# Hybrid decoder step: key norms of sets 1 to 3 by a block of ones and wide reciprocals instead of token-major sums and transpositions

## The chip, the cores and the metric

One Trainium2 chip, one core. The metric is device time in microseconds (us), the median of a few runs.

Engines are named as in the profile: PE multiplies matrices (PEld is its loading of the stationary operand), DVE is the vector engine, ACT the scalar engine, POOL the general-purpose one, SP issues DMAs. Each works through its own list of instructions in order, so an instruction that waits holds up those behind it.

## What is computed

One layer of a decoder for 2048 new tokens and 32 sample tokens (8 sequences of 4), model width 1024, 16 heads of 64 channels. A convolution branch and an RWKV-7 branch share one normalised input. The change is in the RWKV branch, in the keys, which are scaled to unit length per head and token:

```python
kk = (k_f * k_k).reshape(hs)
kk = kk / jnp.maximum(jnp.sqrt(jnp.sum(kk * kk, axis=-1, keepdims=True)), 1e-12)
k_h = (k_f * (1.0 + (a - 1.0) * k_a)).reshape(hs)
...
def step(S, inp):
    r_t, k_t, v_t, d_t, kk_t, a_t = inp
    sa = jnp.einsum('bhvk,bhk->bhv', S, -kk_t)
    S = (S * d_t[:, :, None, :] + sa[..., None] * (kk_t * a_t)[:, :, None, :]
         + v_t[..., None] * k_t[:, :, None, :])
```

`kk` occurs twice in a step, so the kernel multiplies by one over the sum of squares once, in one of the two places.

## The kernel before

**Tiling.** The tokens are cut into four sets of 512 (`th` = 0 to 3). Set 3 (`LAST`) also carries the 32 sample tokens, so its tiles have 544 columns. Channels lie on the 128 partitions, tokens in the columns. A pair `p` = 0 to 7 is two heads, 128 channels. So there are 32 pairs of set and heads, worked one after the other.

**Main stream.** The projections of a set are blocks of 24 matrix products each (`proj`, lines 266 to 276): every fp32 operand is split into a high and a low part of type fp32r, and high times high, low times high and high times low are summed in a PSUM bank called `ip`. In the trace these are `ip<-XH,whl` and `ip<-XL,whl`, one record each. Other products of fp32 operands show as two records each, but for transpositions, which show as one.

**Sides.** For each pair there are generators that run beside the main stream, a piece at a time: `rwkv_keys` (line 808: decays, norms, scaled keys `BK`, receptances `AR`, bonus `bv`), `rwkv_solve` (inverts the triangles `X` of all eight chunks in a chain of small DVE operations), `rwkv_merge`, `rwkv_load`, then `rwkv_chain` (line 1091: eight chunks in series, each PE `pa`, DVE `us`, PE `pb<-us`, DVE and ACT `SV`, PE `pb<-SV`, DVE `S`) and `rwkv_out`. The keys of pair k run while the chain of pair k-1 does.

**What sets the order.** `drive` (line 351) takes a product of the main stream, and then lets each side emit its next pieces where three things hold: its share of the window given to it is due, its inputs and PSUM banks are ready by a modelled clock (class `Clock`, the cost of an instruction in `Traced.cost`, line 130 on), and, for sides not urgent, the modelled DVE is at most 1.8 us ahead of the modelled PE (`BACKLOG`). A `yield` of a side gives the weight of the piece, what its next piece must wait for, and how many banks it needs. So all five engines' orders are fixed when the program is built, and a new cost in the model or a new `yield` can move every piece behind it.

**The norms before.** The squares `sq` (line 821) are multiplied as the stationary operand, 128 tokens at a time, with a two-column matrix `bone2` (line 826). This gives the sums of the two heads with tokens on partitions: `ss`, 128x8. DVE clips and inverts these few numbers (lines 827, 828). Later ACT spreads them over 64 columns each (line 876), PE transposes the four blocks back to channels on partitions (line 880), and DVE multiplies `ta` by them out of PSUM (line 881). In set 3 the 32 sample tokens go the same way apart (lines 829 to 833 and 882 to 889). The matrix `bones` (128x128, ones in two 64x64 blocks) is already there for the bonus (lines 921, 922).

**Buffers.** `tmp` is a pool of 8 tiles of 128x576, shared by the main stream and the sides (line 403); `pt` has two PSUM banks (line 406), `ip` three.

Of the kernel before, what the change touches and what calls it, by code (L numbers as in the profile page):

```python
# [7 lines left out]
F32 = mybir.dt.float32  # L8
F32R = mybir.dt.float32r
BF16 = mybir.dt.bfloat16  # L10
AF = mybir.ActivationFunctionType
ALU = mybir.AluOpType
# [4 lines left out]
P = 128  # L17
# [5 lines left out]
NT = NCH * C  # L23
# [3 lines left out]
W = {"sq": 1.0, "norm": 1.0, "lora": 2.0, "one": 1.0, "scan": 2.0, "exp": 2.0, "key": 1.0, "bones": 1.5,  # L27
     "sv": 1.5, "bt": 2.0, "score": 4.0, "inv0": 5.0, "inv": 0.45, "inv1": 4.0, "merge": 2.0,
     "gk": 1.3, "us": 1.3, "sa": 1.3, "state": 1.3, "samp": 2.0, "gn": 4.0, "out": 2.0}
# [81 lines left out]
class Traced:  # L111
# [18 lines left out]
    def cost(self, op, out, ins, k):  # L130
        n = out.free_size()
        if self.name == "PE":
            if op == "transpose":
                return 109.0
            lhs, rhs = k["lhsT"], k["rhs"]
            if rhs.dtype == F32R:
                mode, t = (P, P), 8 + 0.45 * n
            else:
                part = [next(x for x in (32, 64, 128) if v <= x) for v in (lhs.ap[0][1], lhs.free_size())]
                mode, t = tuple(part), 2 * max(0.84 * max(lhs.free_size(), n), 26.0) / (1 if part == [P, P] else 1.9)  # L140
            t += 170 * (mode != self.clock.mode)
            self.clock.mode = mode
            return t
        if self.name == "DVE":
            per = {"transpose": 1.6, "tensor_tensor_scan": 2.1}.get(op, 1.05)
            if op == "tensor_reduce":
                n = ins[0].free_size()
            return 150 + per * n
        if self.name == "ACT":
            return 200 + 0.84 * n + 90 * max(0, len(ins) - 1)  # L150
        if k.get("op") == ALU.pow:
            return 1650.0
        return 120 + 2.3 * n if op == "tensor_tensor" else 120 + 1.0 * n
# [26 lines left out]
def hybrid_kernel(tc, x_prompt, x_sample, state_conv, state_shift, state_rwkv, norm_g, w_in, conv_w,  # L180
# [5 lines left out]
    V, A, G, T = (Traced(e, n, clock) for e, n in ((nc.vector, "DVE"), (nc.scalar, "ACT"), (nc.gpsimd, "POOL"), (nc.tensor, "PE")))  # L186
# [7 lines left out]
    NSAMP = NS * SL  # L194
# [7 lines left out]
    TW = NT + 64  # L202
# [165 lines left out]
    TPS = NT // P  # L368
# [34 lines left out]
    tmp = ph1.enter_context(tc.tile_pool(name="tmp", bufs=8))  # L403
    ep = ph1.enter_context(tc.tile_pool(name="ep", bufs=2))
    sm = ph1.enter_context(tc.tile_pool(name="sm", bufs=2))
# [399 lines left out]
    def cview(t):  # L805
        return t[:, 0:NT].rearrange("p (c t) -> p c t", t=C)

    def rwkv_keys(th, p, o):

        lt = cur["lora"]  # L810
# [8 lines left out]

        sq = tmp.tile([P, TW], F32, name="tmp")  # L820
        A.activation(out=sq[:, 0:nt], in_=kT[:, 0:nt], func=AF.Square, scale=vc("kk", p))
        yield W["sq"], [sq[:, 0:nt]], 1 + samp
        pt = new_pt([P, 512], F32, name="pt")
        ss = sm.tile([P, 2 * TPS + 2], F32, name="ss")
        for j in range(TPS):
            T.matmul(pt[:, 2 * j:2 * j + 2], lhsT=sq[:, j * P:(j + 1) * P], rhs=bone2, start=True, stop=True)
        V.tensor_scalar(out=ss[:, 0:2 * TPS], in0=pt[:, 0:2 * TPS], scalar1=1e-24, scalar2=None, op0=ALU.max)
        V.reciprocal(ss[:, 0:2 * TPS], ss[:, 0:2 * TPS])
        if samp:
            pt = new_pt([P, 512], F32, name="pt")  # L830
            T.matmul(pt[0:NSAMP, 0:2], lhsT=sq[:, n:nt], rhs=bone2, start=True, stop=True)
            V.tensor_scalar(out=ss[0:NSAMP, 2 * TPS:], in0=pt[0:NSAMP, 0:2], scalar1=1e-24, scalar2=None, op0=ALU.max)
            V.reciprocal(ss[0:NSAMP, 2 * TPS:], ss[0:NSAMP, 2 * TPS:])
        yield W["norm"], [up], 2


        L = tmp.tile([P, TW], F32, name="tmp")
# [33 lines left out]
        kh = tmp.tile([P, TW], F32, name="tmp")  # L871
        A.activation(out=kh[:, 0:nt], in_=ta[:, 0:nt], func=AF.Identity, scale=kah[:, p:p + 1], bias=kai[:, p:p + 1])
        V.scalar_tensor_tensor(out=ta[:, 0:nt], in0=ta[:, 0:nt], scalar=1.0, in1=Pi[:, 0:nt], op0=ALU.add, op1=ALU.mult)

        sb = tmp.tile([P, TW], F32, name="tmp")
        A.copy(sb[:, 0:NT].rearrange("p (a d) -> p a d", d=64), ss[:, 0:2 * TPS].unsqueeze(2).broadcast_to([P, 2 * TPS, 64]))
        yield W["key"], [sb[:, 0:NT]], 1
        pt = new_pt([P, 512], F32, name="pt")
        for j in range(TPS):
            T.transpose(pt[:, j * P:(j + 1) * P], sb[:, j * P:(j + 1) * P], ident)  # L880
        V.tensor_tensor(out=ta[:, 0:n], in0=pt, in1=ta[:, 0:n], op=ALU.mult)
        if samp:
            sb = tmp.tile([P, TW], F32, name="tmp")
            A.copy(sb[0:NSAMP, 0:P].rearrange("p (a d) -> p a d", d=64),
                   ss[0:NSAMP, 2 * TPS:].unsqueeze(2).broadcast_to([NSAMP, 2, 64]))
            yield 0.0, [sb[0:NSAMP, 0:P]], 1
            pt = new_pt([P, 512], F32, name="pt")
            T.transpose(pt[:, 0:NSAMP], sb[0:NSAMP, 0:P], ident[0:NSAMP, 0:NSAMP])
            V.tensor_tensor(out=ta[:, n:nt], in0=pt[:, 0:NSAMP], in1=ta[:, n:nt], op=ALU.mult)
        yield W["key"]  # L890
        V.tensor_tensor(out=kh[:, 0:nt], in0=kh[:, 0:nt], in1=kT[:, 0:nt], op=ALU.mult)
        yield W["key"]
# [730 lines left out]
```

## Time and profile before

| what | value |
|---|---|
| median of 3 runs | 3192.13 us (3189.84 to 3195.04) |
| the profiled execution | 3193.32 us |
| its span, first to last instruction | 3191.6 us |
| mean granted PE clock | 0.992 |
| records on PE, DVE, ACT | 21530, 5704, 2571 |

The page's second part shows the span in 40 slices; a digit is the busy share in tenths:

```profile
PE   7999999999999999999999999999999999999998
PEld 6777777887777778877777789989889889778896
DVE  5687777776666666666666676766677664443332
ACT  5454445444333434434443334344444432211201
POOL 2011111111000001100101010000000000000000
```

Set 0 ends in the ninth slice, set 3 begins near the 24th, and from the 34th on the output products run without the sides. PE shows a 9 nearly everywhere, the others never do. In a row of the timeline stand the start, the duration, the engine, the operation, and output and inputs by name; an idle time in front of it and who ended it follow in brackets. Matrix products overlap at their ends, so what one costs is read from the distance between starts.

### The profile page before, as it was taken

Reading aid. Unit: us, or ns where it says so; the run is one execution under the profiler, and the core shown is the slowest. Engines: PE = TensorE matmul, PEld = TensorE weight load, DVE = VectorE, ACT = ScalarE, POOL = GpSimd, SP = SyncE. Lnnn points to the kernel's source line nnn. Section 1 sums busy time; section 2 is a strip of 40 time slices with the busy share of each in tenths; the row PEclk is TensorE's granted clock in tenths of the full one; section 3 lists DMA queues with packets and bytes.
Section 4 is the critical chain, followed back from the end, with each engine's and each line's share of the span. In section 5 each row is a group of like instructions: output and inputs, shape, how many; then the busy total and the mean of one; then the engine's idle time right before and its main releaser. Section 6 shows DMA issues by size and latency. Waiting matters only on the chain.

```text
span 3191.6 us, 55625 instructions
## 1 busy us (share of the span) xinstructions
PE 3092.0 (97%) x21530; PEld 2596.5 (81%) x21530; DVE 1992.5 (62%) x5704; ACT 1241.9 (39%) x2571; POOL 309.6 (10%) x517
## 2 busy tenths in 40 slices
PE   7999999999999999999999999999999999999998
PEld 6777777887777778877777789989889889778896
DVE  5687777776666666666666676766677664443332
ACT  5454445444333434434443334344444432211201
POOL 2011111111000001100101010000000000000000
PEclk9999999999999999999999999999999999999999
DMA  8786666644444444444444444434443469988863
GB/s 267 258 267 220 213 212 220 207 173 148 146 162 160 155 159 159 169 157 153 159 153 158 159 147 142 138 127 139 144 143 135 138 223 318 363 337 304 316 241 120
DMA packets 241504, 615.09 MB, mean 193 GB/s; under 512 B 33931, under 2 KB 143620, under 8 KB 187479
## 3 DMA queue, kind: packets, MB, share of 16 engines
q1 hardware_dynamic: 241094, 611.00, 55.8%
q8 instruction: 170, 2.79, 0.4%
q14 instruction: 96, 0.78, 0.1%
q0 software_dynamic: 144, 0.52, 0.0%
HBM read 452.10 MB, written 159.36 MB: 192 GB/s over the span
## 4 chain that ended last, share of the span: by engine, by line
PE 69%; DVE 18%; ACT 5%; issue 5%; DMA 3%; POOL 1%; SPq 0%; ACTq 0%; DVEq 0%; POOLq 0%
PE ip L121 49%; PE pt L121 10%; PE po L121 6%; PE pb L121 3%; DVE X L121 2%; DVE tmp L121 2%; DVE tt L121 2%; ACT tmp L121 2%; DVE Mi L121 2%; DVE whl L121 1%; DVE us L121 1%; PE pa L121 1%; DVE S L121 1%; DMA wraw<-in_w_in_dram 1%; ACT Xbd L121 1%
## 5 line engine op out<-in xcount | busy, mean ns | idle before, releaser
L121 PE MATMUL ip<-XH,whl 128*128 128x512 f32 (+3 forms) x7776 | 2105.1, 351 | 6.6 <-DVE gt L121 3.9
L121 PEld LDWEIGHTS ip<-XH,whl 128*128 128x128 f32 x7776 | 1342.0, 190 | 178.3 <-issue 27.5
L121 PE MATMUL ip<-XL,whl 128*128 128x512 f32 (+3 forms) x3888 | 1364.0, 351 | 2.7 <-POOL XL L121 2.6
L121 PEld LDWEIGHTS ip<-XL,whl 128*128 128x128 f32 x3888 | 738.5, 190 | 79.0 <-issue 7.0
L121 DVE TENSOR_TENSOR X<-X,tt 128x60 f32<-128x60 f32 (+24 forms) x992 | 211.7, 213 | 27.5
L121 DVE TENSOR_TENSOR tt<-Mi,X 128x60 f32<-128x60 f32 (+24 forms) x992 | 209.9, 212 | 27.4
L121 DVE SCALAR_TENSOR_TENSOR S<-pb,pe,sp 64x64 f32<-64x64 f32 x512 | 143.8, 281 | 106.6 <-PE pb L121 100.5
L121 ACT ACTIVATE sp<-S,pe 128x128 f32<-128x128 f32 x256 | 99.5, 400 | 244.7 <-DVE S L121 241.2
L121 ACT ACTIVATE tmp<-ip,vec 128x512 f32<-128x512 f32 (+2 forms) x174 | 103.2, 593 | 231.6 <-PE ip L121 230.2
L121 ACT COPY SV<-pb 64x64 f32<-64x64 f32 x256 | 53.3, 208 | 329.2 <-DVE SV L121 325.5
L121 DVE TENSOR_TENSOR whl<-wraw,whl 128x1024 fp32r<-128x1024 f32 x105 | 134.2, 1279 | 58.0 <-ACT whl L121 57.7
L121 PE MATMUL po<-whl,MH 128*128 128x512 f32 x544 | 170.4, 394 | 0.0
L121 DVE TENSOR_TENSOR us<-pa,P 64x64 f32<-64x64 f32 x512 | 110.2, 215 | 45.2 <-PE pa L121 33.7
L121 PEld LDWEIGHTS pb<-us,Xbd 128*128 128x128 f32 x512 | 85.9, 189 | 56.9 <-PE ip L121 21.5
L121 PE MATMUL ip<-RH,whl 128*128 128x512 f32 (+2 forms) x512 | 128.4, 341 | 1.7 <-DMA whl<-w_or 1.6
L121 PEld LDWEIGHTS pb<-SV,BKt 128*128 128x128 f32 x512 | 85.1, 189 | 54.6 <-ACT SV L121 45.9
L121 ACT CAST whl<-wraw 128x1024 fp32r<-128x1024 f32 x105 | 109.5, 1044 | 50.5 <-DMA wraw<-in_w_out_r_dram 14.8
L121 PE MATMUL pb<-SV,BKt 128*128 128x128 f32 x512 | 107.3, 291 | 17.4 <-ACT SV L121 17.3
L121 DVE TENSOR_TENSOR GM<-pt,mask_p 128x512 f32<-128x512 f32 x128 | 82.4, 685 | 64.4 <-PE pt L121 64.4
L121 PEld LDWEIGHTS po<-whl,MH 128*128 128x128 f32 x544 | 102.2, 188 | 24.0 <-DVE whl L121 0.3
L121 PE MATMUL pb<-us,Xbd 128*128 128x64 f32 x512 | 90.1, 258 | 23.7 <-DVE us L121 23.1
L121 ACT COPY Xbd<-Xo 32x256 f32<-32x256 f32 x128 | 88.1, 688 | 64.0 <-DVE Xo L121 61.9
(494 smaller groups left out, 3838.6 us busy)
## 6 DMA issues: line engine op xcount, KB each, us to landing
wraw<-in_w_in_dram SPq DMA_DIRECT2D x81, 512.0 KB
whl<-w_k SPq DMA_DIRECT2D x24, 1024.0 KB
whl<-w_r SPq DMA_DIRECT2D x24, 1024.0 KB
whl<-w_v SPq DMA_DIRECT2D x24, 1024.0 KB
whl<-w_z SPq DMA_DIRECT2D x24, 1024.0 KB
whl<-w_xin SPq DMA_DIRECT2D x24, 1024.0 KB
whl<-w_cg SPq DMA_DIRECT2D x24, 1024.0 KB
whl<-w_zc SPq DMA_DIRECT2D x24, 1024.0 KB
```

What stands on the lines that cost most here:

```text
L121: r = f(*a, **k)
```

## The change

In set 0 the norms stay as they were (`norms_narrow`). From set 1 on (`norms_wide`) the squares are split into an fp32r high part `sh` and a low part `sl`, both are multiplied with `bones`, which gives each channel the sum of its own head's squares, ACT copies the result to SBUF (`ri`), and DVE inverts all 128x512 (544 in set 3) numbers, in pieces of 128 columns. The final multiplication then reads SBUF. The 32 sample tokens need no path of their own. The model of the clock gets a price for the reciprocal.

```diff
+            if op == "reciprocal":
+                per = 6.0
             return 150 + per * n
...
+    def ones_product(pt, h, l, c0, c1, out):
+
+        T.matmul(pt[:, 0:c1 - c0], lhsT=bones, rhs=h[:, c0:c1], start=True, stop=False)
+        T.matmul(pt[:, 0:c1 - c0], lhsT=bones, rhs=l[:, c0:c1], start=False, stop=True)
+        A.copy(out[:, c0:c1], pt[:, 0:c1 - c0])
+
+    def norms_wide(sq, sg, nt, o):
+
+        sh = tmp.tile([P, TW], F32R, name="tmp")
+        A.copy(sh[:, 0:nt], sq[:, 0:nt])
+        yield W["sq"], [sh[:, 0:nt]]
+        sl = tmp.tile([P, TW], F32R, name="tmp")
+        V.scalar_tensor_tensor(out=sl[:, 0:nt], in0=sq[:, 0:nt], scalar=1e-36, in1=sh[:, 0:nt].bitcast(F32),
+                               op0=ALU.max, op1=ALU.subtract)
+        yield W["sq"], [sl[:, 0:nt]], len(sg)
+        ri = tmp.tile([P, TW], F32, name="tmp")
+        for (c0, c1) in sg:
+            ones_product(new_pt([P, 512], F32, name="pt"), sh, sl, c0, c1, ri)
+        yield W["norm"], [ri[:, 0:nt]]
+        for c0 in range(0, nt, P):
+            c1 = min(nt, c0 + P)
+            V.reciprocal(ri[:, c0:c1], ri[:, c0:c1])
+            yield W["norm"] / 2
+        o["ri"] = ri
...
-        yield W["sq"], [sq[:, 0:nt]], 1 + samp
-        pt = new_pt([P, 512], F32, name="pt")
-        ss = sm.tile([P, 2 * TPS + 2], F32, name="ss")
-        for j in range(TPS):
-            T.matmul(pt[:, 2 * j:2 * j + 2], lhsT=sq[:, j * P:(j + 1) * P], rhs=bone2, start=True, stop=True)
-        V.tensor_scalar(out=ss[:, 0:2 * TPS], in0=pt[:, 0:2 * TPS], scalar1=1e-24, scalar2=None, op0=ALU.max)
-        V.reciprocal(ss[:, 0:2 * TPS], ss[:, 0:2 * TPS])
...
-        yield W["norm"], [up], 2
+        if th:
+            yield from norms_wide(sq, sg, nt, o)
+        else:
+            yield from norms_narrow(sq, o)
+        yield 0.0, [up], 2
...
+        if "ri" in o:
+            yield W["key"]
+            V.scalar_tensor_tensor(out=ta[:, 0:nt], in0=o["ri"][:, 0:nt], scalar=1e24, in1=ta[:, 0:nt], op0=ALU.min, op1=ALU.mult)
+        else:
+
             sb = tmp.tile([P, TW], F32, name="tmp")
...
```

The order on PE, where the keys of pair 5 of set 1 begin (the chain with `S_475` is that of pair 4). Before, the four products with `bone2` (128x2, two records each in the trace):

```order
L121 MATMUL pa<-S_475,AR_202 128x128
L121 MATMUL ip<-XL,whl 128x512
L121 MATMUL ip<-XH,whl 128x512
L121 MATMUL pt<-bone_228,tmp 128x2 x4
L121 MATMUL ip<-XH,whl 128x512
L121 MATMUL ip<-XL,whl 128x512
L121 MATMUL ip<-XH,whl 128x512
L121 MATMUL pb<-us,Xbd_208 128x64
```

And, some 30 main products later, the four transpositions:

```order
L121 MATMUL pb<-SV,BKt 128x128
L121 MATMUL ip<-XL,whl 128x512
L121 MATMUL ip<-XH,whl 128x512
L121 MATMUL pt<-ident,tmp 128x128 x4
L121 MATMUL ip<-XH,whl 128x512
```

After the change, at the same place, the two products with `bones` stand one chunk's step later, and no transpositions follow:

```order
L121 MATMUL ip<-XL,whl 128x512
L121 MATMUL pt<-tmp,bones 128x512 x2
L121 MATMUL ip<-XH,whl 128x512
L121 MATMUL pb<-SV,BKt 128x128
L121 MATMUL ip<-XH,whl 128x512
L121 MATMUL ip<-XL,whl 128x512
L121 MATMUL ip<-XH,whl 128x512 x2
L121 MATMUL ip<-XL,whl 128x512
L121 MATMUL ip<-XH,whl 128x512 x2
```

Directly behind these rows on PE comes the chunk's next round, from `pa` to `pb<-us`; it is the stretch in which DVE inverts:

```order
L121 MATMUL pa<-S_475,AR_202 128x128
L121 MATMUL ip<-XL,whl 128x512
L121 MATMUL ip<-XH,whl 128x512 x2
L121 MATMUL ip<-XL,whl 128x512
L121 MATMUL ip<-XH,whl 128x512 x2
L121 MATMUL pt<-lora,up 128x512 x2
L121 MATMUL ip<-XL,whl 128x512
L121 MATMUL pb<-us,Xbd_208 128x64
```

So between `pb<-SV` and `pb<-us` there stand fourteen main products, `pa` and the two products `pt<-lora,up`. On DVE, the same round of the chain before:

```order
L121 TENSOR_TENSOR us<-pa,P_11045 64x64 x2
L121 TENSOR_SCALAR ss<-pt 128x8
L121 RECIPROCAL ss<-ss 128x8
L121 COPY SV<-pb 64x64
L121 SCALAR_TENSOR_TENSOR S_475<-pb,pe,sp 64x64 x2
L121 SCALAR_TENSOR_TENSOR tmp<-rst,tmp 128x512
L121 TENSOR_TENSOR us<-pa,P_11045 64x64 x2
```

and after the change (the first row is the low part `sl`, `tmp<-rst,tmp` is a scan of the decays):

```order
L121 SCALAR_TENSOR_TENSOR tmp<-tmp 128x512
L121 TENSOR_TENSOR us<-pa,P_11035 64x64 x2
L121 COPY SV<-pb 64x64
L121 SCALAR_TENSOR_TENSOR S_475<-pb,pe,sp 64x64 x2
L121 RECIPROCAL tmp<-tmp 128x128 x3
L121 TENSOR_TENSOR us<-pa,P_11035 64x64 x2
L121 RECIPROCAL tmp<-tmp 128x128
L121 COPY SV<-pb 64x64
L121 SCALAR_TENSOR_TENSOR tmp<-rst,tmp 128x512
```

Three of the four reciprocals now stand between `S` and the `us` that the next `pb` of the chain needs, and the scan has moved behind that `us`.

More of the change, by code (lines that the diff above doesn't have):

```diff
@@ L806, in cview, with norms_narrow @@
         return t[:, 0:NT].rearrange("p (c t) -> p c t", t=C)
+    def ones_product(pt, h, l, c0, c1, out):
[19 more added lines that the diff above has]
+        o["ri"] = ri
+    def norms_narrow(sq, o):
+        yield W["sq"], [sq[:, 0:NT]], 1
+        pt = new_pt([P, 512], F32, name="pt")
+        ss = sm.tile([P, 2 * TPS], F32, name="ss")
+        for j in range(TPS):
+            T.matmul(pt[:, 2 * j:2 * j + 2], lhsT=sq[:, j * P:(j + 1) * P], rhs=bone2, start=True, stop=True)
+        V.tensor_scalar(out=ss, in0=pt[:, 0:2 * TPS], scalar1=1e-24, scalar2=None, op0=ALU.max)
+        V.reciprocal(ss, ss)
+        yield W["norm"]
+        o["ss"] = ss
     def rwkv_keys(th, p, o):
@@ L821, in rwkv_keys @@
         A.activation(out=sq[:, 0:nt], in_=kT[:, 0:nt], func=AF.Square, scale=vc("kk", p))
-        yield W["sq"], [sq[:, 0:nt]], 1 + samp
-        pt = new_pt([P, 512], F32, name="pt")
-        ss = sm.tile([P, 2 * TPS + 2], F32, name="ss")
-        for j in range(TPS):
-            T.matmul(pt[:, 2 * j:2 * j + 2], lhsT=sq[:, j * P:(j + 1) * P], rhs=bone2, start=True, stop=True)
-        V.tensor_scalar(out=ss[:, 0:2 * TPS], in0=pt[:, 0:2 * TPS], scalar1=1e-24, scalar2=None, op0=ALU.max)
-        V.reciprocal(ss[:, 0:2 * TPS], ss[:, 0:2 * TPS])
[L829 to L833, printed above, removed]
-        yield W["norm"], [up], 2
+        if th:
[3 more added lines that the diff above has]
+        yield 0.0, [up], 2
         L = tmp.tile([P, TW], F32, name="tmp")
@@ L873, in rwkv_keys @@
         V.scalar_tensor_tensor(out=ta[:, 0:nt], in0=ta[:, 0:nt], scalar=1.0, in1=Pi[:, 0:nt], op0=ALU.add, op1=ALU.mult)
[L875 to L882, printed above, removed]
+        if "ri" in o:
+            yield W["key"]
+            V.scalar_tensor_tensor(out=ta[:, 0:nt], in0=o["ri"][:, 0:nt], scalar=1e24, in1=ta[:, 0:nt], op0=ALU.min, op1=ALU.mult)
+        else:
             sb = tmp.tile([P, TW], F32, name="tmp")
-            A.copy(sb[0:NSAMP, 0:P].rearrange("p (a d) -> p a d", d=64),
-                   ss[0:NSAMP, 2 * TPS:].unsqueeze(2).broadcast_to([NSAMP, 2, 64]))
-            yield 0.0, [sb[0:NSAMP, 0:P]], 1
+            A.copy(sb[:, 0:NT].rearrange("p (a d) -> p a d", d=64), o["ss"].unsqueeze(2).broadcast_to([P, 2 * TPS, 64]))
+            yield W["key"], [sb[:, 0:NT]], 1
             pt = new_pt([P, 512], F32, name="pt")
-            T.transpose(pt[:, 0:NSAMP], sb[0:NSAMP, 0:P], ident[0:NSAMP, 0:NSAMP])
-            V.tensor_tensor(out=ta[:, n:nt], in0=pt[:, 0:NSAMP], in1=ta[:, n:nt], op=ALU.mult)
+            for j in range(TPS):
+                T.transpose(pt[:, j * P:(j + 1) * P], sb[:, j * P:(j + 1) * P], ident)
+            V.tensor_tensor(out=ta[:, 0:n], in0=pt, in1=ta[:, 0:n], op=ALU.mult)
         yield W["key"]
```

## The prediction

> **What bounds the kernel now.** I read the page first, then what PE waited for, then windows of about one pair's length, then the timeline around the instructions that change.
>
> ```profile
> span 3191.6 us, 55625 instructions
> ...
> PE 3092.0 (97%) x21530; PEld 2596.5 (81%) x21530; DVE 1992.5 (62%) x5704; ACT 1241.9 (39%) x2571; POOL 309.6 (10%) x517
> ```
>
> PE works 97% of the span and is idle for 3191.6 - 3092.0 = 99.6 us. DVE is 38% idle. So time comes off by taking work from PE, and goes on by making PE wait. What makes it wait, in the answer on PE's waits:
>
> ```profile
> PE pb L121 <- DVE us L121: 23.1, 39, 1.6
> PE pb L121 <- ACT SV L121: 17.3, 29, 1.4
> ```
>
> These two are the chain, 40.4 us in 68 waits over 32 pairs. It is the one part of the program where PE stands waiting for a result of DVE again and again, so a busier DVE would show here. Three windows of 87 us tell how closely the two are coupled (columns: window, length, then busy time and count of PE, PEld, DVE, ACT, POOL; clock, DMA share, GB/s):
>
> ```profile
> 1519.00:1606.00 87.00, 86.04 (x589) 67.73 (x584) 50.76 (x152) 35.59 (x74) 10.45 (x18) 1.00 0.46 155
> 1606.00:1693.00 87.00, 86.06 (x544) 67.14 (x543) 54.20 (x162) 36.11 (x76) 7.82 (x16) 1.00 0.45 158
> ...
> 2302.00:2389.00 87.00, 85.21 (x761) 78.68 (x761) 64.25 (x217) 37.11 (x91) 7.33 (x12) 1.00 0.43 147
> ```
>
> The first two are set 2, the third is set 3. From 50.76 to 54.20 us of DVE PE loses nothing; from 54.20 to 64.25 it loses 86.06 - 85.21 = 0.85 us, 0.085 us for each us of DVE.
>
> **PE's work, removed and added.** Here are the removed groups and the group whose form is added, in a pair of set 1 (columns: start, duration; `bone` is the token-major sum, `ident,tmp` the transpositions, `bones` the bonus, which has the very form of the new norm product):
>
> ```profile
> 1070.58 0.40 PE L121 MATMUL ip<-XH,whl 128*128 128x512 f32 x1
> 1070.81 0.95 PE L121 MATMUL pt<-bone,tmp 128*128 128x2 f32 x8
> 1071.62 0.48 PE L121 MATMUL ip<-XH,whl 128*128 128x512 f32 x1
> 1071.94 0.40 PE L121 MATMUL ip<-XL,whl 128*128 128x512 f32 x1
> ...
> 1081.29 0.60 PE L121 MATMUL pt<-ident,tmp 128*128 128x128 f32 x4
> 1081.65 0.48 PE L121 MATMUL ip<-XH,whl 128*128 128x512 f32 x1
> 1081.96 0.39 PE L121 MATMUL ip<-XL,whl 128*128 128x512 f32 x1
> ...
> 1094.52 0.63 PE L121 MATMUL pt<-tmp,bones 128*128 128x512 f32 x2
> 1094.98 0.39 PE L121 MATMUL ip<-XH,whl 128*128 128x512 f32 x1
> 1095.22 0.38 PE L121 MATMUL pa<-S,AR 128*128 128x128 f32 x2
> ```
>
> A main product costs 1070.81 - 1070.58 = 0.23 us. The sums cost 1071.94 - 1070.81 - 0.23 = 0.90 us; the main product behind them took 0.32 instead of 0.23, and that is in it. The transpositions cost 1081.96 - 1081.29 - 0.23 = 0.44. The two `bones` products cost 1095.22 - 1094.52 - 0.23 = 0.47. So a pair of sets 1 and 2 sheds 0.90 + 0.44 - 0.47 = 0.87 us, and sixteen of them 13.9 us.
>
> Set 3 sheds more, since the sample tokens had two small products and a transposition of their own:
>
> ```profile
> 2036.99 0.30 PE L121 MATMUL ip<-XL,whl 128*128 128x288 f32 x1
> 2037.12 0.75 PE L121 MATMUL pt<-tmp,bones 128*128 128x512 f32 x4
> 2037.73 0.38 PE L121 MATMUL ip<-XH,whl 128*128 128x288 f32 x1
> 2037.94 0.39 PE L121 MATMUL pb<-SV,BKt 128*128 128x128 f32 x2
> ...
> 2088.37 1.05 PE L121 MATMUL pt<-bone,tmp 128*128 128x2 f32 x8
> 2089.28 0.38 PE L121 MATMUL ip<-XL,whl 128*128 128x288 f32 x1
> 2089.59 0.22 PE L121 MATMUL pt<-bone,tmp 128*32 128x2 f32 x2
> 2089.74 0.53 PE L121 MATMUL ip<-XH,whl 128*128 128x288 f32 x2
> 2090.11 0.38 PE L121 MATMUL pt<-Xbd,sq 128*128 128x128 f32 x2
> ```
>
> A main product of 288 columns costs 2037.12 - 2036.99 = 0.13 us. The sums: 2090.11 - 2088.37 = 1.74 less three such products, 1.35 us. The transpositions of the 512 tokens as above, 0.44; that of the 32 I set at 0.25, a little over half of it. New: 2037.94 - 2037.12 - 0.13 = 0.69. So 1.35 + 0.44 + 0.25 - 0.69 = 1.35 us, times eight is 10.8. Together PE sheds **24.7 us**. A check by groups, whose busy times leave out some of the gaps:
>
> ```profile
> L121 PE MATMUL pt<-bone,tmp 128*128 128x2 f32 (+1 forms) x272 | 32.3, 239 | 0.0
> L121 PE MATMUL pt<-ident,tmp 128*128 128x128 f32 (+1 forms) x168 | 25.9, 271 | 0.0
> L121 PE MATMUL pt<-tmp,bones 128*128 128x512 f32 (+1 forms) x80 | 21.8, 363 | 0.0
> ```
>
> Of 272 records 208 go (the 64 of set 0 stay): 24.7 us. Of 168 transpositions 104 go (4 in each of 24 pairs, and 8): 16.0. `bones` gets 64 more records, 17.4 at the group's mean. That is 23.3 us. I take **24**.
>
> **DVE's work.** Per pair, from these rows (mean ns behind the bar's busy time):
>
> ```profile
> L121 DVE TENSOR_TENSOR tmp<-tmp 128x512 fp32r<-128x512 f32 x24 | 28.5, 1188 | 8.6 <-ACT tmp L121 8.2
> ...
> L121 DVE TENSOR_TENSOR tmp<-pt,tmp 128x512 f32<-128x512 f32 x40 | 27.5, 687 | 2.2 <-PE pt L121 1.3
> ...
> L121 DVE SCALAR_TENSOR_TENSOR tmp<-tmp 128x512 f32<-128x512 f32 x24 | 16.4, 682 | 0.2
> ...
> L121 DVE RECIPROCAL ss<-ss 128x8 f32<-128x8 f32 x32 | 6.3, 197 | 0.7
> ...
> L121 DVE TENSOR_TENSOR tt<-Mi,X 128x8 f32<-128x8 f32 x32 | 5.4, 169 | 0.7
> L121 DVE TENSOR_SCALAR ss<-pt 128x8 f32<-128x8 f32 x32 | 5.3, 165 | 26.5 <-PE pt L121 26.5
> ```
>
> and, from the view of the tile `ss`, the shortest, the median and the longest reciprocal of both shapes:
>
> ```profile
> L121 DVE RECIPROCAL ss<-ss x40: 100/200/204, 63.8 to 2503.4; 128x8 f32<-128x8 f32 x32, 32x2 f32<-32x2 f32 x8
> ```
>
> Gone are 0.165 + 0.197 + 0.687 = 1.05 us. Added are `sl` (0.68, or 1.19 as the bonus's low part takes, which has its form), the last multiplication (0.68) and four reciprocals of 128 columns, which nothing in the trace shows. Their bounds: 8 columns took 28 ns more than the `TENSOR_TENSOR` of 8, so about 3.5 + 1 ns a column, and 0.20 + 120 x 0.0045 = **0.74 us** for 128; or, with the shortest 32x2 reciprocal at 100 ns, (197 - 100) / 6 = 16 ns a column, and **2.14 us**. I take 0.9, near the lower end, because a short instruction of any other kind here also takes 165 ns and more, so that most of the 197 is not per column. DVE then gets 0.9 + 0.68 + 3.6 - 1.05 = **4.1 us** a pair, 99 us in all, of its 1199 idle ones. Were it all paid at the slope above, it would be 99 x 0.085 = 8.4 us; by the two windows of set 2 it would be nothing.
>
> **Where a reciprocal meets the chain.** In the order three of them stand between `S` and `us`. The time PE has there, from the rows of the same stretch in another pair:
>
> ```profile
> 924.27 1.13 PE L121 MATMUL pt<-lora,up 64*128 64x512 f32 x4
> ...
> 925.66 0.38 PE L121 MATMUL pb<-SV,BKt 128*128 128x128 f32 x2
> 926.08 0.58 DVE L121 SCALAR_TENSOR_TENSOR S<-pb,pe,sp 64x64 f32<-64x64 f32 x2 [2.70 <-PE pb L121]
> ...
> 928.20 0.45 DVE L121 TENSOR_TENSOR us<-pa,P 64x64 f32<-64x64 f32 x2
> ```
>
> PE: fourteen main products at 0.23, the two `lora` products 1.13, `pb` and `pa` about 0.3 each, 4.95 us from `pb<-SV` to `pb<-us`. DVE: `S` starts 0.42 behind that `pb` and takes 0.58, `us` 0.45, so 1.45 us and three reciprocals. These are late only from (4.95 - 1.45) / 3 = **1.17 us** each on. At 0.9 there are 0.8 us to spare.
>
> [...]
>
> **The rest, costed at nothing.** ACT casts `sh` and copies `ri` where it spread `ss`: one operation more a pair, under PE's products, with ACT 39% busy; if that cover failed, the new products would be emitted later, not PE stopped. `tmp` gives out two more of its eight tiles a pair; a tile that comes free late would hold up ACT's evacuation of `ip`, for which three banks are cover. SP and POOL issue what they did. PE's main products keep their order; by the order the keys' last product stands some 20 main products later in most pairs, but the next pair's chain starts at the same main product as before, so nothing is forced. I put what PE loses to all of this and to the chain at **4 us**, the middle between nothing and 8.4.
>
> The sum against the profiled execution: 3193.3 - 24 + 4 = 3173.3 us (its span 3191.6 and 1.7 around it). The median shown is 1.2 us below that execution, so **3172 us**.
>
> **Rivals.** *The saving is partly paid back in the chain.* For it: DVE is the one that the chain waits for, and keys and chain share it in the same third of a pair. Against it: the model of the clock prices the reciprocal, and PE's order leaves 0.8 us. One wait of 0.5 us more in each of 24 pairs gives 3184. *The reciprocal is dear, and the chain stops PE.* At the upper bound of 2.14 us, three of them are late by 3 x (2.14 - 1.17) = 2.9 us, 70 us over 24 pairs, and the time is 3172 - 4 + 70 = 3238. It turns the change into a loss when 3 x (r - 1.17) exceeds the 1.0 us that PE sheds a pair, so from r = 1.5 us on. The 8-column row speaks against it. *PE's relief isn't worth time*, because PE would only wait longer for the chain that it now reaches sooner: 3192. Against it: PE waited for the chain only 40.4 us in 32 pairs.
>
> **Chances.** The forecast (3164 to 3180) 0.62; part paid back (3180 to 3192) 0.23; no relief (about 3192) 0.06; dear reciprocal (3195 to 3238) 0.09. A measurement of this kernel can tell 0.2%, 6.4 us, from no change: faster than 3185.7 takes the first case and most of the second, 0.80; within it 0.12; slower 0.08. The range leaves out the last two cases and the end of the second, 0.18 in all: 3164 to 3190.
>
> **What would show it.** In the profile after: PE's busy time down by 23 to 25 us; a `RECIPROCAL` group of 128x128 with a mean of 0.74 to 0.95 us; DVE's busy time up by 85 to 110 us; PE's waits for `us` and `SV` at 40 to 50 us. A mean above 1.2 us, or those waits at 60 us and more, would prove me wrong, and so would a span that keeps its length with PE's busy share below 97%.

## The result: 29 us slower, and the profile after

| kernel | median of its runs | ratio to before, 95% interval |
|---|---|---|
| before | 3192.13 us | |
| changed | 3221.40 us (3216.86 to 3226.11, 5 runs) | 1.0092 [1.0078, 1.0107] |

The change costs 29 us where 20 were forecast as a gain. The profiled executions have nearly the same granted PE clock, 0.992 before and 0.993 after, so the clock as a whole doesn't explain it. The page of the changed kernel (its profiled execution took 3216.86 us):

```profile
span 3215.1 us, 55238 instructions
...
PE 3069.3 (95%) x21282; PEld 2571.1 (80%) x21282; DVE 2067.8 (64%) x5760; ACT 1260.6 (39%) x2595; POOL 312.2 (10%) x517
```

PE sheds 3092.0 - 3069.3 = 22.7 us, as forecast. But its idle time goes from 99.6 to 3215.1 - 3069.3 = 145.8 us, 46.2 more. 3193.3 - 22.7 + 46.2 is the profiled time. What PE waits for now (total, times, longest):

```profile
PE pb L121 <- DVE us L121: 23.1, 30, 1.6
PE pb L121 <- ACT SV L121: 16.9, 28, 1.2
PE pt L121 <- DVE Yc L121: 15.0, 17, 1.2
PE pa L121 <- DVE S L121: 12.4, 18, 1.1
PE pt L121 <- ACT SV L121: 10.6, 11, 1.0
```

The chain's two waits are as long as before, where they were 23.1 and 17.3 us. New are waits for a `pt` bank (`Yc`, `SV`), which before came to 0.6 us and none, and the wait of `pa` for `S` (1.9 before). These three make up 36 of the 46 us. The reciprocal itself, in the groups by form (busy, mean ns):

```profile
L121 DVE RECIPROCAL tmp<-tmp 128x128 f32<-128x128 f32 x96 | 84.2, 921 | 15.9 <-ACT tmp L121 15.1
```

It takes 0.92 us, as assumed.

**Where the time is lost.** The 12570 records that write `ip` stand in nearly the same sequence in every kernel here (at most 58 differ), so the start of the n-th can be compared between traces. From record 3200 to record 6300 lie 12 pairs of sets 1 and 2; I call them the steady stretch. Its windows, first of the kernel before, then of the changed one (length, then busy time and count of PE, PEld, DVE, ACT, POOL; clock, DMA share, GB/s):

```profile
959.27:1864.51 905.24, 892.85 (x5998) 711.09 (x5996) 577.42 (x1753) 363.94 (x764) 94.53 (x172) 1.00 0.45 157
```

```profile
954.90:1886.03 931.13, 884.16 (x5840) 701.67 (x5839) 609.70 (x1796) 373.58 (x776) 96.62 (x172) 0.99 0.44 152
```

PE works 8.7 us less there and idles 47.0 instead of 12.4 us: 25.9 us lost, 2.2 us a pair, nearly all that the change costs. The granted clock is a little lower in this stretch, 0.99 instead of 1.00. What is lost is idle time all the same, 34.6 us of it against the 8.7 that PE works less.

**What happens at a pair's end.** The timeline of one pair's end before (start, duration, engine; in brackets the idle time in front and who ended it):

```profile
1045.75 1.15 PE L121 MATMUL pt<-SV,GM 128*64 128x64 f32 x32
...
1046.83 0.66 PE L121 MATMUL pt<-ident,vT 128*128 128x128 f32 x4
...
1047.53 1.17 ACT L121 COPY SV<-pt 64x512 f32<-64x512 f32 x2 [0.98 <-PE pt L121]
...
1048.73 0.68 DVE L121 TENSOR_TENSOR Yc<-pt,Yc 128x512 f32<-128x512 f32 x1
...
1049.80 2.81 ACT L121 COPY Xbd<-Xo 32x256 f32<-32x256 f32 x4 [1.10 <-DVE Xo L121]
...
1050.81 0.60 PE L121 MATMUL pt<-ident,BK 128*128 128x128 f32 x4
...
1054.83 0.21 PE L121 MATMUL pt<-T,GM 32*32 32x32 f32 x1
```

The same place in the changed kernel:

```profile
1047.89 1.15 PE L121 MATMUL pt<-SV,GM 128*64 128x64 f32 x32
...
1048.98 0.65 PE L121 MATMUL pt<-ident,vT 128*128 128x128 f32 x4
...
1050.46 0.45 DVE L121 STREAM_TRANSPOSE Xo<-X 128x256 f32<-128x256 f32 x1
1050.93 0.69 DVE L121 TENSOR_TENSOR Yc<-pt,Yc 128x512 f32<-128x512 f32 x1
1050.94 2.76 ACT L121 COPY Xbd<-Xo 32x256 f32<-32x256 f32 x4 [5.70 <-DVE Xo L121]
...
1051.68 0.66 PE L121 MATMUL pt<-ident,BK 128*128 128x128 f32 x4 [1.12 <-DVE Yc L121]
...
1053.70 1.17 ACT L121 COPY SV<-pt 64x512 f32<-64x512 f32 x2
...
1054.93 0.21 PE L121 MATMUL pt<-T,GM 32*32 32x32 f32 x1 [0.96 <-ACT SV L121]
```

There are two `pt` banks, used in turn. The own rows (`pt<-SV,GM`) take one and DVE empties it into `Yc`; the load (`pt<-ident,vT`) takes the other and ACT empties it into `SV`. Before, PE wants the first bank back (`pt<-ident,BK`) 5.06 us after the own rows, and DVE is there after 2.98. In the changed kernel the chain ends later on PE, so these own rows come late, and PE arrives at `pt<-ident,BK` 1051.68 - 1.12 - 1047.89 = 2.67 us after them. DVE needs 3.04, and 0.69 for the operation: PE waits. On ACT the copies `Xbd<-Xo` now stand ahead of `SV<-pt`. ACT stands idle for 5.70 us until the triangles are inverted, then copies them for 2.76, and so holds the second bank until 1054.87; `pt<-T,GM`, at 1054.93, has waited for it.

The wait of `pa` for `S` comes from the same move, in the stretch of the keys. The rows of DVE and PE there in the changed kernel:

```profile
1003.76 1.22 DVE L121 TENSOR_TENSOR_SCAN tmp<-rst,tmp 128x512 f32<-128x512 f32 x1 [0.61 <-ACT tmp L121]
...
1005.02 1.15 ACT L121 ACTIVATE tmp<-tmp 128x512 f32<-128x512 f32 x2 [0.48 <-DVE tmp L121]
...
1005.75 0.75 DVE L121 SCALAR_TENSOR_TENSOR AR<-kT,nkk,tmp 128x512 f32<-128x512 f32 x1 [0.77 <-ACT tmp L121]
...
1006.42 0.59 DVE L121 SCALAR_TENSOR_TENSOR S<-pb,pe,sp 64x64 f32<-64x64 f32 x2
...
1007.07 0.49 PE L121 MATMUL pa<-S,AR 128*128 128x128 f32 x2 [0.81 <-DVE S L121]
```

`S` is queued on DVE behind `AR`. `AR` waits 0.77 us for ACT's exponentials, and these wait for the scan. No reciprocal stands there.

### The profile page after: what moved, and what is told of

It reads as the page before. It is cut to its first block, busy times and chain, and to the rows that moved or that the text cites. A ratio compares the mean times of both kernels' runs of the same rounds, so it can differ in the third digit from the quotient of the medians.

```text
span 3215.1 us, 55238 instructions
## 1 busy us (share of the span) xinstructions
PE 3069.3 (95%) x21282; PEld 2571.1 (80%) x21282; DVE 2067.8 (64%) x5760; ACT 1260.6 (39%) x2595; POOL 312.2 (10%) x517
## 4 chain that ended last, share of the span: by engine, by line
PE 50%; DVE 16%; ACT 5%; issue 4%; DMA 1%; POOL 0%; DVEq 0%; ACTq 0%; POOLq 0%; SPq 0%
PE ip L121 35%; PE pt L121 7%; PE po L121 6%; DVE X L121 4%; DVE tt L121 3%; DVE tmp L121 2%; PE pb L121 2%; ACT tmp L121 1%; ACT Xbd L121 1%; DVE Mi L121 1%; DVE S L121 1%; PE pa L121 1%; ACT Mc L121 1%; DVE us L121 1%; ACT SV L121 0%
## 5 line engine op out<-in xcount | busy, mean ns | idle before, releaser
L121 PE MATMUL ip<-XH,whl 128*128 128x512 f32 (+3 forms) x7776 | 2096.6, 351 | 10.8 <-DVE gt L121 5.8
L121 ACT ACTIVATE sp<-S,pe 128x128 f32<-128x128 f32 x256 | 99.6, 400 | 259.1 <-DVE S L121 258.0
L121 PEld LDWEIGHTS pa<-S,AR 128*128 128x128 f32 x512 | 86.3, 188 | 40.9 <-DVE S L121 30.3
```

Source lines behind the costliest of these rows:

```text
L121: r = f(*a, **k)
```

## The experiments

Theory A: the order costs. The keys are emitted later, and with them the load and the chain's end, and the pair's end jams as above. Theory B: the 3.7 us that DVE spends on reciprocals in each pair slow the chain. Other theories are named where they occur.

**e1: reciprocals of one column.** The reciprocals' time is taken away and the order kept (127 of 128 columns are left out of the inversion):

```diff
-            V.reciprocal(ri[:, c0:c1], ri[:, c0:c1])
+            nc.vector.reciprocal(ri[:, c0:c0 + 1], ri[:, c0:c0 + 1])
+            clock.add("DVE", [ri[:, c0:c1]], [ri[:, c0:c1]], 150 + 6.0 * (c1 - c0))
```

> The changed kernel with every reciprocal cut to one column of its 128; the model of the clock still charges the full price, so that the order of all engines stays that of the changed kernel. Left out: the inversion of 127 of 128 columns, and so the key norms are not those of the reference. Theory A (the order: the chain, the keys' scores and the load now fall together at the end of a pair, and two `pt` banks are held while DVE and ACT work on the triangles): the wait of `pa` for `S` beside the reciprocals goes (0.8 us a pair), the waits of `pt` for `Yc` and for `SV` at the pair's end stay at 9 us and more each, and the time is 3198 to 3212. Theory B (the 3.7 us a pair that DVE spends on inverting slow the chain): all the new waits go and the time is 3165 to 3175.

Measured 3222.08 us, ratio 1.0093 [1.0078, 1.0108]. The reciprocals of e1 in the groups by form:

```profile
L831 DVE RECIPROCAL tmp<-tmp 128x1 f32<-128x1 f32 x104 | 8.8, 148 | 15.5 <-ACT tmp L121 15.2
```

75 us of DVE are gone and nothing is gained. Theory B falls. Of PE's waits in the steady stretch the two at `pt` stay, as theory A has it (11.2 and 9.0 with the full reciprocals):

```profile
PE pt L121 <- DVE Yc L121: 10.2, 10, 1.1
PE pt L121 <- ACT SV L121: 8.9, 9, 1.0
```

The time is 10 us above theory A's range. Its detail on `pa` was wrong: the wait for `S` stays at 8.8 us in the steady stretch (7.7 with the full reciprocals), which sent me to the rows above.

**e2: the reciprocals without the change.** In the kernel before, in each pair of sets 1 to 3, once each after `Pi`, `kh`, `BK` and the bonus's product are made:

```diff
+    def extra(th, p, src):
+        if th:
+            nc.vector.reciprocal(GMB[(th * NB + p) % 2][:, 0, 0], src if len(src.ap) > 2 else src.rearrange("p (h t) -> p h t", t=64))
...
+        extra(th, p, Pi[:, 0:P])
...
```

> The kernel before with four additional reciprocals of 128 columns in each pair of sets 1 to 3, written to a buffer that is idle there and not told to the model of the clock, so that the order of before stays. Theory A: DVE has room for them, waits of `pt` for `Yc` and `SV` stay below 5 us each, and the time is 3192 to 3207, with whatever is lost lost in the chain's own waits (`us`, `S`). Theory B: about as much is lost as in the changed kernel beside its relief of 23 us, 3215 to 3250.

Measured 3198.94 us, ratio 1.002 [1.001, 1.003]. DVE gets 69.3 us more (2061.8 against 1992.5) and the time grows by 6 to 8: 0.1 us for each us of DVE, near the 0.085 of the prediction. In the steady stretch nothing is lost (903.67 us); set 3, where DVE is busiest, lost 6.2. The load, the own rows and the merge stand on PE where they stood before; but on DVE many of the keys' rows changed places, and single steps of the chain stand up to 4 main products later in the steady stretch.

**e3: the merge held until the triangles are ready.**

```diff
         GM, Xo, Mo = (o[k] for k in ("GM", "Xo", "Mo"))
+        yield 0.0, [Xo]
         Xbd = o["Xbd"] = XB[(th * NB + p) % 2]
```

> The changed kernel with one more wait of the order-maker: the merge gives out its first piece only when the inverted triangles Xo are ready, so that on ACT the copies of the load (`SV<-pt`) come ahead of the copies of the triangles (`Xbd<-Xo`), as they did before the change. Theory A: the wait of `pt` for ACT's `SV` (10.6 us in 11 waits) goes, 1 us a pair, and the time is 3200 to 3210; the wait of `pt` for `Yc` stays. Theory B: no change, 3217 to 3226.

Measured 3221.13 us, ratio 1.0097 [1.0082, 1.0112]: as a whole it misses theory A's range and lies in theory B's. In the steady stretch it did what was expected: 918.56 us instead of 931.13, and the wait of `pt` for `SV` (9.0 us there) is gone. But against the changed kernel it lost more elsewhere, 12.5 us in set 0, where the order moved as well, and 5.7 from set 3 on. Theory B isn't borne out by that, since it had no place for a gain in the steady stretch.

**e4: no price for the reciprocal in the model.**

```diff
-            if op == "reciprocal":
-                per = 6.0
```

> The changed kernel without the reciprocal's price in the model of the clock: the same instructions, ordered as if each reciprocal took 0.28 us. The load and the chain then stand at the pair's end where they stood before the change. Theory A: the pair's end runs as before, the waits of `pt` for `Yc` and `SV` fall below 5 us each, and the time is 3172 to 3195, with at most 0.8 us a pair lost where the chain meets reciprocals that the order did not allow for. Theory B: DVE has the same work and the order allows less for it, 3220 to 3245.

Measured 3194.65 us, ratio 1.0009 [1.0000, 1.0019]. The instructions are those of the changed kernel, and 27 of the 29 us are back. The load, the merge and all but one of the groups of own rows in the steady stretch stand on PE where they stood before the change. PE's waits at `pt` in all:

```profile
PE pt L121 <- DVE Yc L121: 4.8, 9, 1.5
...
PE pt L121 <- ACT SV L121: 1.0, 1, 1.0
```

Theory A holds, at the upper end of its range.

**e5: the old instructions, ordered late.** The kernel before, with extra pieces and charges on the model's clock alone (8.0 ns a column where the changed kernel's price is 6.0):

```diff
+        if th:
+            yield W["sq"], [sq[:, 0:nt]]
+            clock.add("DVE", [sq[:, 0:nt]], [sq[:, 0:nt]], 150 + 1.05 * nt)
         yield W["sq"], [sq[:, 0:nt]], 1 + samp
...
-        yield W["norm"], [up], 2
+        if th:
+            yield W["norm"], [ss[:, 0:2 * TPS]]
+            for c0 in range(0, nt, P):
+                clock.add("DVE", [ss], [ss], 150 + 8.0 * min(P, nt - c0))
+                yield W["norm"] / 2
+        yield 0.0 if th else W["norm"], [up], 2
```

> The kernel before, with its own narrow norms and no wide reciprocal, ordered late: in sets 1 to 3 the norms are cut into as many pieces as in the changed kernel and the model of the clock is charged for work that is not there, until the keys' scores, the load and the end of the chain stand 3.7 to 4.4 us of main products later on PE and the copies `Xbd<-Xo` stand ahead of `SV<-pt` on ACT, as in the changed kernel, in sets 1 and 2. Theory A (the order costs): about as much is lost as in the changed kernel, without its relief of 0.74 us a pair: 16 pairs at 2 to 2.9 us, 3222 to 3238, with PE waiting for `Yc` and for `SV` at `pt` 9 us and more each. Theory C (the order is harmless, and only together with the new instructions does it cost): 3188 to 3197.

Measured 3256.83 us, ratio 1.0204 [1.0190, 1.0218]. Not one wide reciprocal, and 65 us lost, more than either theory's range. In the steady stretch it is 30.1 us (935.32), which theory A gives; set 3 lost another 25, which it didn't. The waits in the steady stretch of e5:

```profile
PE pa L121 <- DVE S L121: 15.9, 22, 1.3
PE pt L121 <- ACT SV L121: 7.3, 11, 0.7
```

The jam is there, but with another split: more at `pa`, 0.5 us at `Yc`. The order isn't quite that of the changed kernel: in most pairs the load and the first own rows stand 22 main products later than before, in the changed kernel 17. So a late order costs by itself; which wait takes the loss depends on details that I didn't separate.

**e6: wide norms in set 3 alone.** As e4, with

```diff
-        if th:
+        if samp:
             yield from norms_wide(sq, sg, nt, o)
```

> The wide norms in set 3 alone, without the reciprocal's price in the model of the clock; sets 1 and 2 as before the change. In set 3 the changed kernel without that price gained 11.6 us on the kernel before by the start of the same main products, and in sets 1 and 2 it lost some 5. If gains and losses of the sets are separate: 3176 to 3183. If the end of set 3 gives it back, where the chain of the last pairs stands later: 3187 to 3193.

Measured 3199.33 us, ratio 1.0024 [1.0015, 1.0032], worse than both ranges. The order in set 3 isn't that of e4, though the instructions there are; e14 takes this up.

**e7: own rows in a bank of `pa`.**

```diff
-        pt = new_pt([P, 512], F32, name="pt")
+        pt = ps_a.tile([P, 4, P], F32, name="pa").rearrange("p a b -> p (a b)")
```

> The changed kernel with the own rows of a pair (`pt<-SV,GM`, read by DVE as `Yc`) in a bank of `pa` in place of one of the two `pt` banks. Theory A: the wait of `pt` for `Yc` goes (11.2 us in the 12 steady pairs of sets 1 and 2, 15.0 in all), and as the load's `SV<-pt` then has the other bank to itself, the wait behind it shrinks as well: 3197 to 3208. If the two banks only name the wait and the true limit is DVE's and ACT's rows at the pair's end: the waits move to the next product, 3215 to 3224.

Measured 3245.28 us, ratio 1.0170 [1.0153, 1.0187], worse than either side expected. In its steady stretch the wait of `pt` for `Yc` is gone, 11.2 us in the changed kernel, and that for `SV` has grown from 9.0 to 18.4 us: PE only arrives earlier at the bank that ACT holds. The second theory was right in kind. A part of the time is the granted clock: it was 0.985 to 0.988 in the four runs, and 0.991 to 0.994 in those of the kernel before beside them. If PE's time goes with it, 0.6% of 3245 us is an estimated 19 of the 54 us. In the steady stretch PE is idle for 44.6 us, 2.4 less than in the changed kernel, but busy 5.7 us more, at a clock of 0.98 instead of 0.99. Set 3 lost 11.5 us on the kernel before, for a reason that I didn't follow.

**e8: both of e3 and e7.**

> The changed kernel with both: the own rows in a bank of `pa`, and the merge's first piece held until the inverted triangles are ready, so that the load's copies come ahead of the triangles' on ACT in most pairs. Theory A: both waits of the pair's end go, 2 us in each of the 12 steady pairs, and what stays is the wait of `pa` for `S` (0.7 us a pair): 3193 to 3203. If the waits move to the next product: 3212 to 3224.

Measured 3213.77 us, ratio 1.0068 [1.0052, 1.0084]. The waits in its steady stretch:

```profile
PE pa L121 <- DVE S L121: 9.4, 12, 1.0
...
PE pt L121 <- ACT SV L121: 1.5, 1, 1.5
```

Both waits of the pair's end are gone but for 1.5 us, and the stretch takes 911.96 us: 19 of the 26 us are back there. What stays is mostly `pa`. The whole misses theory A's range and lies in that of the other theory, though the waits didn't move: set 3 and what follows lost 19.5 us on the kernel before, 17 more than the changed kernel did. The profiled execution was the slowest of four, 6 us above their median, and its clock in set 3 was 0.99 where the changed kernel's was 1.00.

**e9 and e10: the wide norms in the keys' old pieces.** With the price (e9), and without (e10):

```diff
-        yield W["sq"], [sh[:, 0:nt]]
+        yield W["sq"] / 2, [sh[:, 0:nt]]
...
-        yield W["sq"], [sl[:, 0:nt]], len(sg)
+        yield W["sq"] / 2, [sl[:, 0:nt]], len(sg)
...
-        for c0 in range(0, nt, P):
-            c1 = min(nt, c0 + P)
-            V.reciprocal(ri[:, c0:c1], ri[:, c0:c1])
-            yield W["norm"] / 2
-        o["ri"] = ri
+        o["ri"], o["cuts"] = ri, [(c0, min(nt, c0 + P)) for c0 in range(0, nt, P)]
...
+        invert(o, 0)
         yield W["lora"]
...
+        invert(o, 1)
         yield W["one"], [L[:, 0:nt]]
...
```

> The changed norms with the reciprocal's full price in the model of the clock, but cut into the keys' old pieces: the two halves of the square's split carry half a weight each, the four reciprocals ride one each on the pieces of the decays (lora, one, scan, exp) and carry no weight, so that the sum of the keys' weights is that of the kernel before. In sets 1 and 2 the chain, the load and the merge then stand on PE where they stood before, in set 3 up to 12 us apart. Theory A: the waits of the pair's end stay away in sets 1 and 2, and the stretch of 12 steady pairs takes 905.2 - 8.9 + 4 = 898 to 902 us where it took 905.2 before and 931.1 after; in all 3172 to 3190, the rest by what set 3 does. If the price itself or the DVE time costs: 3200 and more.

> The same without the reciprocal's price in the model of the clock. The order is nearly the same in sets 1 and 2, other in set 3. Theory A: the steady stretch takes 898 to 902 us, as with the price; the whole 3172 to 3190. A difference between the two of more than 6 us would come from set 3 alone.

Measured 3198.53 us, ratio 1.0027 [1.0016, 1.0039], and 3200.37, ratio 1.0032 [1.0019, 1.0044], both above the range. The steady stretch takes 901.92 and 903.31 us, shorter than before the change: the same price that went with a loss of 26 us there now goes with a gain of 3. The gain is lost where the order still moved, in the first pairs of set 1 and behind set 3. In the first pairs (8.0 us lost in e9) the granted clock was 0.97 where it was 1.00 before, and PE's idle time grew by only 3.0 us; behind set 3 (9.8 us lost) it is idle time. In all seven runs of e9 the clock was 0.989 to 0.991, and 0.992 to 0.996 in those of the kernel before beside them. That is 0.3%, an estimated 10 us if PE's time goes with it, and as much as the whole loss. So e9's loss can't be put down to waits alone.

**e11 and e12: only where the order stands still.** As e9, with `range(10, 29)` (e11) or `range(10, 24)` (e12) in place of all pairs from set 1 on, and the narrow norms with their sample path elsewhere:

```diff
-        if th:
+        if th * NB + p in range(10, 24):
             yield from norms_wide(sq, sg, nt, o)
```

> The wide norms in the pieces of the kernel before, with the reciprocal's price, for 19 pairs: pair 2 of set 1 to pair 4 of set 3. The first two pairs of set 1 and the last three of set 3 keep the narrow norms, since in the run with all pairs the time gained was lost there again (11.7 us in the first two, 12.7 us in the last). Outside of pairs 0 to 4 of set 3 the chain, the load and the merge stand where they stood before the change. If order is what decides: 3.3 us gained in the 12 steady pairs, 0.5 in the two beside them, some 5 to 7 in set 3: 3180 to 3185. If the ends lose again whatever the order there: 3188 to 3196.

> The same for the 14 pairs from pair 2 of set 1 to the end of set 2 alone: the chain, the load and the merge stand on PE where they stood before in every pair of all sets, and the scores 1.4 us later in those 14. What the wide norms are worth with the order held still: by the steady stretch of the run with all pairs 14 x 0.28 = 4 us, so 3185 to 3189. If PE's relief of 0.74 us a pair came through whole: 3181. If it is worth nothing: 3191.

Measured 3190.94 us, ratio 1.0010 [1.0000, 1.0019], and 3189.27, ratio 0.9995 [0.9986, 1.0004]. e11 misses the first range and lies in the second, though not for the second's reason: the ends lost next to nothing, and the five pairs of set 3 with another order gave the gain back. e12 as a whole can't be told from the kernel before. It comes nearest to the change itself, since the load stands on PE where it stood before in every pair, and the own rows and the merge in all but one. The order isn't wholly still: in the 12 steady pairs half of the chain's `pa` products stand later, by up to 16 main products, and the keys' scores by up to 6. The window and the longest wait of its steady stretch:

```profile
960.75:1862.32 901.57, 880.85 (x5877) 700.93 (x5876) 604.70 (x1789) 371.12 (x776) 93.90 (x172) 1.00 0.46 157
...
PE pb L121 <- DVE us L121: 12.1, 19, 0.9
```

Against the window of before PE works 12.0 us less, and idles 20.7 instead of 12.4. Two thirds of what PE sheds, 0.7 us a pair, are paid back even here. The wait for `us`, 3.0 us in the same stretch before, is now 12.1; `Wm` adds 4.9 us, and the wait for `SV` falls from 8.3 to 2.3. The rows tell what stands in front of `us`. Nine of its waits, 8.1 us together, are of this kind:

```profile
1029.21 2.06 DVE L121 STREAM_TRANSPOSE Mi<-Mc 128x1024 f32<-128x1024 f32 x1 [0.62 <-ACT Mc L121]
...
1031.31 0.45 DVE L121 TENSOR_TENSOR us<-pa,P 64x64 f32<-64x64 f32 x2
...
1031.90 0.41 PE L121 MATMUL pb<-us,Xbd 128*128 128x64 f32 x2 [0.89 <-DVE us L121]
```

Before, the two stand the other way round:

```profile
1027.80 0.45 DVE L121 TENSOR_TENSOR us<-pa,P 64x64 f32<-64x64 f32 x2
...
1028.27 2.08 DVE L121 STREAM_TRANSPOSE Mi<-Mc 128x1024 f32<-128x1024 f32 x1
```

So 0.9 us a pair is once more an order that moved, on DVE. Nine other waits, of 0.41 us each, come directly behind three reciprocals and the scan, which keep DVE busy from 1001.26 to 1004.92 without a gap in the first of these pairs. That much, at most, can be put down to the reciprocals; no run cut them in this order.

**e13 and e14: does set 3 follow its order?** e14 has e6's instructions and e6's order in sets 1 and 2, and one number of the planner changed; `norms_heavy` stands for the changed kernel's `norms_wide`, its reciprocals charged without the price. e13 has e12's 14 pairs besides:

```diff
+            if p == 0:
+                weight["keys"] += 3.0
+            yield from norms_heavy(sq, sg, nt, o)
```

> Wide norms in 22 pairs: 14 of sets 1 and 2 in the old pieces and with the price (as in e12), and all eight of set 3 as in e4: in pieces of their own with extra weight, without the price. The chain, the load and the merge then stand in sets 1 and 2 where they stood in the kernel before and in set 3 exactly where they stood in e4. If the order decides, the parts add up: 3.7 us gained in the 12 steady pairs and 10.4 - 2.4 = 8 in set 3 and behind it, 3176 to 3183. If set 3's 10.4 us were chance or depend on what went before: 3186 to 3194.

> e6 (the wide norms in set 3 alone, without the price) with one number changed: the planner's sum of weights for the keys is raised by 3.0 at the first pair of set 3, where e6 learned that sum only a pair later. The instructions are those of e6, and the order in set 3 is that of e4. If the order decides: 8 us faster than the kernel before and 14 faster than e6, 3181 to 3187. If not: as e6, 3194 to 3202.

Measured 3183.93 us, ratio **0.9978 [0.9969, 0.9988]**, and 3188.53, ratio 0.9984 [0.9974, 0.9993]. The order decides: e14 and e6 have the same instructions, and one number of the planner makes 0.4% between them. Between records 6300 and 10000 e6 lost 13 us on e14, 6 of them idle time of PE; the clock in that stretch was 0.99 in e6 and 1.00 in e14. e13 is faster than both kernels, some 7 us below the kernel before and 37 below the changed one. Both times lie 1 to 1.5 us above the ranges expected.

The time of each stretch against the kernel before, from the starts of `ip` records 0, 2400, 3200, 6300, 10000 and 12569 in the traces (us; the first column holds the same instructions up to the end of set 0, and most of its -5.2 to +1.7 goes with the granted clock, see the last section):

| | set 0 | first pairs of set 1 | 12 steady pairs | to record 10000 (set 3) | the rest |
|---|---|---|---|---|---|
| changed | -5.2 | +1.1 | +25.9 | -2.1 | +4.5 |
| e4 | +0.7 | -0.1 | +4.1 | -10.4 | +2.4 |
| e5 | -0.6 | +4.6 | +30.1 | +25.1 | +7.3 |
| e6 | -2.2 | 0.0 | 0.0 | +2.2 | +5.9 |
| e9 | -4.7 | +8.0 | -3.3 | -7.0 | +9.8 |
| e12 | +1.7 | -0.1 | -3.7 | -1.5 | -0.2 |
| e13 | +0.3 | +1.4 | -3.2 | -10.9 | +6.3 |
| e14 | +1.0 | 0.0 | -1.0 | -11.0 | +7.0 |

Where set 3 has e4's order (e13 and e14 but for its first pair), it gains 10.4, 10.9 and 11.0 us. PE is idle there for 14.5 to 14.8 us, and for 15.5 before, at a clock of 1.00 in all four: in this order PE's relief in set 3, 10.8 us in the prediction, comes through.

## Why the prediction was wrong

**What bounds the kernel** was right: PE, whose busy and idle time add up to the loss.

**PE's relief** was right: 22.7 us for 24, at nearly the same granted clock.

**The reciprocal** was right: 0.92 us for 0.9. That was a choice between bounds of 0.74 and 2.14 us, and the 4.5 ns a column behind the lower one was too small: the two means give (921 - 197) / 120 = 6.0 ns a column. Most of the 197 ns isn't per column, as argued: cut to one column (e1) a reciprocal takes 148. But the 165 ns set as the least of the short instructions of other kinds is too high, since a `TENSOR_SCALAR nw<-fin` of one column takes 149 in the mean.

**DVE's work** was sized too high, 75.3 us for 99. Part of it is the low part of the bonus, whose mean fell from 1188 to 689 ns, 24 x 0.5 = 12 us: in 14 of its 24 places before it started during a POOL operation and took 1.52 to 1.73 us, in the changed kernel it does so in none and takes 0.68 to 0.73 (last section). Another 4 us is that the records of reciprocals in a row overlap (three, from 998.64 us on in the changed kernel's trace, take 2.58 together): 96 x 0.921 = 88.4 us, and the group is busy for 84.2. I didn't follow the rest.

**Where a reciprocal meets the chain** was right for the changed kernel: the waits for `us` and `SV` at `pb` are 40.0 us, in the range of 40 to 50, and cutting the reciprocals (e1) gains nothing. The slope of 0.085 was near what e2 gave, but it compared a window of set 2 with one of set 3, whose work on PE differs; that it fits is partly luck.

**The step that failed** is "The rest, costed at nothing", and in it the sentence that "the next pair's chain starts at the same main product as before, so nothing is forced", with the 4 us put on it. PE's additional idle time was 46.2 us. That the chain starts at the same product is so. But in most pairs of the steady stretch the chain's end and the keys' scores stand 20 main products (4.7 us) later on PE, and the load 17 (4.0), while the own rows, the load and the merge share two banks at the pair's end. The prediction had seen the 20 products at the keys and took them for harmless. I looked at the one place of the order that hadn't moved and concluded for the rest. The order to read was that of the bank's readers: on ACT `Xbd<-Xo` stands ahead of `SV<-pt`, an instruction that waits for the end of the inversion ahead of one that frees a bank. That alone isn't the whole (e3): `Yc` and `S` on DVE come late as well, and only with both banks freed (e8) were 19 of the 26 us back.

Behind it stands a second oversight: I took the model of the clock as speaking for the change, since it prices the reciprocal. For the load and the merge of the steady stretch to stay in place, either that price had to go (e4) or the extra pieces with their weights (e9); it took both to move them. And the model's prices for other work are off: `Traced.cost` charges 200 + 0.84 x 256 = 415 ns for a copy `Xbd<-Xo`, and the trace has 2.76 / 4 = 690. That this is why the planner saw no jam is argued and wasn't tried.

**The rivals.** "The saving is partly paid back in the chain" (3184, one wait of 0.5 us a pair) is near what e12 shows behind the reciprocals, 0.41 us in nine of 12 pairs; e12's other wait, of 0.9 us, was in no rival. "PE's relief isn't worth time" came to 3192, near e4 in number only, for in set 3 of e4 the relief came through. The loss of 29 us was in none of them: the dear reciprocal, my slow case, had the wrong mechanism.

## What to carry to other kernels

Where a planner lays the order, a change of the work and a change of the order are two changes: hold the order still, and time each alone, before either is judged. Whether it was still is read from the records of every engine: e12's PE looked still, and DVE had swapped two instructions. When pieces move, look on each engine at what now stands in front of the instructions that free a shared bank, above all at one that waits for the end of a long chain (here ACT stood idle for 5.70 us in front of `Xbd<-Xo`). A wait taken away at one bank may only lengthen that at the next: in e7 11.2 us went at the one, and the other's 9.0 became 18.4. Here the holders of both had to be moved together (e8, 1.5 us left).

## What the hardware showed besides

**DVE and POOL.** The low part of the bonus on DVE (`tmp<-tmp`, fp32r) beside POOL's `cv<-cv,tmp`, before:

```profile
1091.47 1.28 POOL L121 TENSOR_TENSOR cv<-cv,tmp 128x512 f32<-128x512 f32 x1 [12.73 <-DVE tmp L121]
1091.78 1.53 DVE L121 TENSOR_TENSOR tmp<-tmp 128x512 fp32r<-128x512 f32 x1
```

and in the changed kernel:

```profile
1092.15 0.68 DVE L121 TENSOR_TENSOR tmp<-tmp 128x512 fp32r<-128x512 f32 x1
1092.31 1.66 POOL L121 TENSOR_TENSOR cv<-cv,tmp 128x512 f32<-128x512 f32 x1 [9.81 <-DVE tmp L121]
```

In the two traces whichever of these two starts second takes longer: DVE in 14 places before (1.52 to 1.73 us instead of 0.68), POOL in one place before and in ten of the changed kernel (1.66 us instead of 1.28). In the first two rows DVE ends 0.56 us behind POOL, little less than the 0.68 us it takes where it starts first; in the other two POOL ends 1.14 us behind DVE, little less than its 1.28.

**The same instructions, 4 us apart.** Between records 400 and 800, in set 0, thirteen of the kernels have the same work in the same order. The window of the kernel before:

```profile
104.55:232.98 128.43, 123.22 (x767) 96.33 (x766) 95.71 (x258) 64.82 (x113) 13.71 (x19) 0.95 0.79 249
```

and of the changed one:

```profile
104.42:228.74 124.32, 119.41 (x768) 93.21 (x767) 94.92 (x258) 64.12 (x113) 13.43 (x19) 0.99 0.81 254
```

Ten of the thirteen traces show a clock of 0.95 here and take 128.1 to 128.9 us; three (changed, e6, e9) show 0.99 and take 124.1 to 124.9. So two profiles can differ by 4 us with nothing changed, and the clock column tells when they do. In the traces of the kernel before and of the changed one the granted clock falls to 0.50 for 3.41 to 10.24 us at a time and is 1.00 between the falls. One fall in e7's steady stretch:

```profile
1130.19:1133.60 3.41, 1.13 (x35) 0.91 (x35) 1.46 (x4) 3.31 (x6) 0.00 (x0) 1.00 0.89 305
1133.60:1137.01 3.41, 3.41 (x11) 2.30 (x9) 1.52 (x3) 2.51 (x6) 1.58 (x2) 0.50 0.02 7
```

PE was idle for 2.3 of the 3.41 us before it. The stretch has seven falls, and PE was idle for 1.6 to 2.7 us of the 3.41 us before each; the same stretch has one fall before the change, two in the changed kernel and none in e12. Whether a wait brings on a fall was not shown: no run here tests it.
